# Attention layer: the root mean square of later queries and keys by a product with ones

## The chip, the cores and the metric

The kernel runs on one core of one Trainium2 chip. The metric is the device time of one execution in microseconds (us). The core has five engines that each work through a fixed list of instructions in order: TensorE (PE, matrix products; PEld is its weight load), VectorE (DVE), ScalarE (ACT), GpSimd (POOL), and SyncE (SP), which issues the loads and stores. They wait for each other by semaphores.

## What is computed

Two layers with d = 1024 over 512 latent tokens and 256 context tokens (T = 768). Layer 0 mixes tokens by grouped-query attention with 16 query heads and 4 key heads of 64 elements, layer 1 by a bidirectional state space scan; each is followed by a gated FFN. The change is in layer 0's attention:

```python
def rms_norm(x, g):
    y = x * lax.rsqrt(jnp.mean(x * x, axis=-1, keepdims=True) + EPS)     # EPS = 1e-6
    return y * g

q_l, k_l, v_l = jnp.split(h_lat @ w_qkv, [Q_DIM, Q_DIM + KV_DIM], axis=-1)
q_l = rms_norm(q_l.reshape(bsz, seq, N_HEADS, HEAD_DIM), q_norm)         # HEAD_DIM = 64
k_l = rms_norm(k_l.reshape(bsz, seq, N_KV_HEADS, HEAD_DIM), k_norm)
q_l, k_l = apply_rope(q_l, cos, sin), apply_rope(k_l, cos, sin)
...
s = einsum(q, k) * HEAD_DIM ** -0.5        # latent queries: all keys; context queries: context keys
o = softmax(s) @ v
```

So each query and key vector of 64 elements is scaled by the inverse root of its mean square, and its latent part is rotated by cos and sin. The result must be accurate to float32.

## The kernel before

Activations lie transposed: features on the 128 partitions, tokens along the free axis. A tile of queries holds two heads (64 partitions each) by 768 tokens, a tile of keys two key heads. Products that need float32 accuracy are done with a high and a low part (hi is a rounded copy made on ScalarE, lo the rest from VectorE or GpSimd: `split`, L85 and L87) and three products.

A *unit* is one such tile of queries or keys on its way from the projection to the scores. There are ten: keys 0 and 1, queries 0 to 7. Queries 0 to 3 and both keys come from projections in an earlier stage (tiles `raw`), queries 4 to 7 are projected in the unit itself (`queries`, tiles `qs`). The elementwise engine of a unit is given by `eng`: VectorE for keys 0 and queries 0, GpSimd for the other eight. The function `normed` does a unit's norm and rotation:

- ScalarE squares the tile (`qsq`, L523) and multiplies it by the gain (L524); four loads on SP's queue make a copy with rows exchanged in blocks of 32 (`qsw`, L527); `eng` does the rotation in three 512-wide steps (L528 to L530).
- `rstd_rows` (L226) then has PE multiply each 128 tokens of the squares with two indicator columns (`ssq`, six products, tokens on the partitions), VectorE and ScalarE form the inverse root on 128 x 12 elements (L239 to L244, one step of Newton behind Ln and Exp), VectorE spreads it over 128 x 768 (`rbq`, L247), PE transposes that in six pieces (`rsTq`, L253, four and two), and VectorE multiplies the tile with them (L534, 512 and 256).
- Queries end with hi (`qh`, ScalarE, L85) and lo (`ql`, VectorE, L87), keys with hi and lo copies for both halves of the partitions (L545 to L548).

The heads run as eight *pairs* (`Pair`), some 30 us each, from about 118 to 384 us. A pair has seven steps t: PE scores (`ps_s`, L668 with the correction `diag`, L670), ScalarE's exponential (`pr`, L671), VectorE's sum of exponentials (`acc`, `accc`), PE's products with the values one step later (`ps_o`, L632), at the end the sums with a tile of ones (`ps_sum`, `ps_oc`, L638), their inverse and the output (L641 to L645). In its steps the next pair's maxima are prepared too (`ps_m`, L596, reduced on VectorE, L598), and at its end these become the next pair's `diag` (`mz` L614, L619); so `qh` of pair p + 1 is needed in the first step of pair p's maxima run, which is the step t = 0 of pair p.

`ps_s` and `ps_m` share two PSUM buffers of two banks each; all other products (`Bk`) rotate through single banks.

Between the steps `Fill.run` (L182) pulls work from a list of generators, in the order queries 1, 2, 3, one ada, keys 1, query 4, and so on (`"123a4k5a6a7aaa"`, where `a` is a piece of the modulation, `ps_ada` and `ps_adt`). A generator yields an estimate of PE time, or `BREAK`, which costs 1 and rests it for three steps. `fill.require(qgen[p + 1])` at a pair's start runs what is left of the next queries. The program order that comes out is then placed on each engine by a scheduler, which keeps each engine's list in the order in which it expects the instructions to be ready.

The weights that are split during the heads (`wst`, `wh`, `wl`, and `wada` for the modulation) share one set of ten buffers of 128 x 1024 (`t4`), so a load on SP can wait for the reader of an older one.

Of the kernel before, what the change touches and what calls it, by code (L numbers as in the profile page):

```python
# [7 lines left out]
P = 128  # L8
F32 = mybir.dt.float32
F32R = mybir.dt.float32r  # L10
AF = mybir.ActivationFunctionType
ALU = mybir.AluOpType
# [5 lines left out]
L = 512  # L18
C = 256
T = L + C  # L20
HD = 64
# [4 lines left out]
EPS = 1e-6  # L26
# [41 lines left out]
def t3(g, name, dt=F32, n=T):  # L68
    return g.t3p.tile([P, n], dt, tag="t3", bufs=g.n3, name=name)
# [6 lines left out]
def _r(ap):  # L76

    return ap.bitcast(F32)


def split(g, src, hi, lo, lo_engine="dve", pin=False):

    nc = g.nc
    keep = g.tc.keep_in_program_order if pin else lambda i: i
    keep(nc.scalar.copy(hi, src))  # L85
    eng = nc.vector if lo_engine == "dve" else nc.gpsimd
    keep(eng.tensor_tensor(lo, src, _r(hi), ALU.subtract))  # L87
# [85 lines left out]
BREAK = object()  # L173
# [53 lines left out]
def rstd_rows(g, sq, n, cols, width, name, bank):  # L227

    nc = g.nc
    c = cols.shape[-1]
    nt = n // P
    ps = bank(f"ss{name}")
    for t in range(nt):
        nc.tensor.matmul(ps[:, t * c : (t + 1) * c], sq[:, t * P : (t + 1) * P], cols, start=True, stop=True)
    small = lambda nm: g.p.tile([P, nt * c], F32, tag="rst", bufs=8, name=nm)
    a, y, u = small("rsa"), small("rsy"), small("rsu")
    nc.vector.tensor_scalar(a, ps[:, : nt * c], 1.0 / width, EPS, ALU.mult, ALU.add)  # L239

    for f in ((lambda: nc.scalar.activation(y, a, AF.Ln)), (lambda: nc.scalar.activation(y, y, AF.Exp, scale=-0.5))):
        follow(g, f()) if g.tables else f()
    nc.vector.tensor_tensor(u, y, a, ALU.mult)
    nc.vector.scalar_tensor_tensor(u, y, -0.5, u, ALU.mult, ALU.mult)  # L244
    rb = t3(g, f"rb{name}", n=n)
    wide = lambda v: v.unsqueeze(2).broadcast_to([P, nt * c, P // c])
    nc.vector.scalar_tensor_tensor(rb.rearrange("p (a b) -> p a b", b=P // c), wide(u), 1.5, wide(y), ALU.add, ALU.mult)  # L247
    yield BREAK
    out = []
    for t0 in range(0, nt, 4):  # L250
        pt = bank(f"rsT{name}")
        for t in range(t0, min(nt, t0 + 4)):
            nc.tensor.transpose(pt[:, (t - t0) * P : (t - t0 + 1) * P], rb[:, t * P : (t + 1) * P], g.ident)  # L253
        yield (pt, t0 * P, min(n, (t0 + 4) * P))
# [124 lines left out]
def attention(g, fill, X, late):  # L379


    nc, I = g.nc, g.I
    S64 = slice(0, 64), slice(64, 128)
    Bk, Sb = (lambda name: Bank(g, name)), (lambda name: S(g, name))
# [48 lines left out]
    for m in range(KT):  # L433
        sq = t2("sql") if m else acc
# [7 lines left out]
    e = g.p.tile([P, 2 * KT], F32, name="silu")  # L442
# [20 lines left out]
    for m in range(KT):  # L463
# [5 lines left out]
        if m in (1, 2):  # L469
            for a in range(4 * m - 4, 4 * m):  # L470
                sq = t2("sqc")[:, :C] if a else sqc
# [35 lines left out]
    def values():  # L507
        for t in range(T // P):
# [7 lines left out]
                yield 0.32  # L516
            nc.scalar.copy(vt[t], ps[:, :256])


    def normed(qs, gain, eng):  # L520

        sq = t3(g, "qsq")
        nc.scalar.activation(sq, qs, AF.Square)  # L523
        nc.scalar.activation(qs, qs, AF.Identity, scale=gain)  # L524
        sw = t2("qsw")
        for b in range(4):
            nc.sync.dma_start(sw[32 * (b ^ 1) : 32 * (b ^ 1) + 32], qs[32 * b : 32 * b + 32, :L])  # L527
        eng.tensor_tensor(qs[:, :L], qs[:, :L], g.cos, ALU.mult)  # L528
        eng.tensor_tensor(sw, sw, g.sin, ALU.mult)
        eng.tensor_tensor(qs[:, :L], qs[:, :L], sw, ALU.add)  # L530
        for r in rstd_rows(g, sq, T, g.blk, HD, "q", Bk):
            if r is not BREAK:
                pt, c0, c1 = r
                nc.vector.tensor_tensor(qs[:, c0:c1], qs[:, c0:c1], pt[:, : c1 - c0], ALU.mult)  # L534
            yield BREAK
# [16 lines left out]
    qprep = {}  # L552

    def queries(p, qs, eng):
        if qs is None:
            w = load_w(g, I["wq"][p - 4], lo_engine="pool")
            yield BREAK
            qs = t3(g, "qs")
            for h, c0, n in ((hc, L, C), (hl, 0, L)):
                ps = Bk("ps_q")  # L560
                for k in range(KT):
                    ks = slice(k * P, (k + 1) * P)
                    mm3(g, (w[0][:, ks], w[1][:, ks]), [(ps[:, :n], h[k])], k == 0, k == KT - 1)
                    yield 3 * n / 2400
                nc.scalar.copy(qs[:, c0 : c0 + n], ps[:, :n])
            yield BREAK
        yield from normed(qs, g.qn8, eng)
        qprep[p] = t3(g, "qh", F32R), t3(g, "ql", F32R)
        split(g, qs, *qprep[p])
        yield 0  # L570

    onesr = g.const.tile([P, P], F32R, name="onesr")
# [6 lines left out]
    class Pair:  # L579
# [43 lines left out]
        def steps(self):  # L623

            (qh, ql), (kh, kl) = qprep[self.p], k2[self.kv]
            po = acc = None
            o = g.t3p.tile([P, T], F32, tag="o", bufs=2, name=f"o{self.p}")

            def values(po, pr, t, off, n, first, last):
                v = vt[t][:, self.kv * HD : (self.kv + 1) * HD]  # L630
                for e in range(2):
                    nc.tensor.matmul(po[S64[e], :n], v, pr[:, 512 * e + off : 512 * e + off + n], start=first, stop=last)  # L632

            def final(po, ps, acc, out):

                n = out.shape[-1]
                for e in range(2):
                    nc.tensor.matmul(ps[S64[e], :n], g.ones[:, :HD], acc[:, n * e : n * e + n], start=True, stop=True)  # L638
                y, u = t2("y")[:, :n], t2("u")[:, :n]

                nc.scalar.activation(y, ps, AF.Ln)  # L641
                nc.scalar.activation(y, y, AF.Exp, scale=-1.0)
                nc.vector.tensor_tensor(out, po, y, ALU.mult)
                nc.vector.scalar_tensor_tensor(u, ps, -1.0, y, ALU.mult, ALU.mult)
                nc.vector.scalar_tensor_tensor(out, u, 2.0, out, ALU.add, ALU.mult)  # L645

            def later_lat(po, pr, t, acc):
                values(po, pr, t, 0, L, t == 0, t == 5)
                if t == 5:
                    final(po, Bk("ps_sum"), acc, o[:, :L])  # L650

            def later_ctx(pr, acc):
                pc = Bk("ps_oc")
                for t in range(2):
                    values(pc, pr, 4 + t, C * t, C, t == 0, t == 1)
                final(pc[:, :C], pc[:, C:], acc, o[:, L:])
                if self.p < 6:
                    nc.sync.dma_start(odram[self.p], o)

            prev = None  # L660
            for t in range(7):
                ps, pr = Sb("ps_s"), g.t3p.tile([P, 1024], F32, tag="pr", bufs=3, name="pr")
                for q0, n, k0, off in (((0, L, t * P, 0),) if t < 6 else ((L, C, L, 0), (L, C, L + P, C))):
                    q, k = slice(q0, q0 + n), slice(k0, k0 + P)
                    outs = [ps[:, 512 * e + off : 512 * e + off + n] for e in range(2)]
                    for i, (a, b) in enumerate(((kh, qh), (kl, qh), (kh, ql))):
                        for e in range(2):
                            nc.tensor.matmul(outs[e], a[S64[e], k], b[S64[e], q], start=i == 0, stop=False)  # L668
                    for e in range(2):
                        nc.tensor.matmul(outs[e], onesr[S64[e]], self.diag[S64[e], q], start=False, stop=True)  # L670
                nc.scalar.activation(pr, ps, AF.Exp)  # L671
                if t == 0:
                    po = Bk("ps_o")
                elif t == 1:
                    acc = g.t3p.tile([P, 1024], F32, tag="acc", bufs=1, name="acc")
                    nc.vector.tensor_tensor(acc, prev, pr, ALU.add)
                elif t < 6:
                    nc.vector.tensor_tensor(acc, acc, pr, ALU.add)
                else:
                    acc = t2("accc")  # L680
                    halves = pr.rearrange("p (e k q) -> p e k q", e=2, k=2)
                    nc.vector.tensor_tensor(acc.rearrange("p (e q) -> p e q", e=2), halves[:, :, 0], halves[:, :, 1], ALU.add)
                prev = pr
                yield (lambda t=t, pr=pr, po=po, acc=acc: later_lat(po, pr, t, acc)) if t < 6 else (
                    lambda pr=pr, acc=acc: later_ctx(pr, acc))
            g.o.append(o)

    early = []
    for n, j in enumerate((0, 1, 2, 4, 5, 3)):
        ps = Bk("ps_c")  # L690
# [750 lines left out]
```

## Time and profile before

| | |
|---|---|
| Time, median of 3 runs | 1910.94 us (1908.98 to 1913.17) |
| Time of the profiled execution | 1905.24 us |
| Its span | 1903.5 us |
| TensorE busy | 1866.1 us (98%), 10796 products |
| VectorE busy | 1308.4 us (69%) |
| ScalarE busy | 822.8 us (43%) |
| GpSimd busy | 313.7 us (16%) |
| First scores of pairs 0 and 1 | 117.83 and 147.44 us |

Times in the profile are from one execution, in us unless ns is given, and L12 is line 12 of the kernel. A row of the groups reads: line, engine, operation, output and inputs, shapes, count, then busy time, mean ns of one, and the idle time of the engine before them with what ended it. A piece of the chain of waits reads: start, duration, engine, tile, line, count. In a row of waits stand the waiting engine and line, what it waited for, and total, times and longest.

### The profile page before, as it was taken

The numbers are of one execution on the slowest core, as the hardware profiler recorded it, in microseconds if no ns is written. First come the engines' busy times: TensorE is split into PE (matmuls) and PEld (weight loads), VectorE is DVE, ScalarE is ACT, GpSimd is POOL, SyncE is SP. The second block draws the span as 40 slices with busy tenths as digits, with TensorE's granted clock in tenths as the row PEclk, the third lists the DMA queues.
The fourth block names the chain that finished last, engine by engine and source line by source line (L and its number), as shares of the span: only waits on it lengthen the run. The fifth ranks groups of instructions, "written<-read, shape, count | busy, mean of one in ns | idle before, by whom it ended". The sixth has DMA issues, their size and how long they took to land.

```text
span 1903.5 us, 27436 instructions
## 1 busy us (share of the span) xinstructions
PE 1866.1 (98%) x10796; PEld 1540.9 (81%) x10796; DVE 1308.4 (69%) x1943; ACT 822.8 (43%) x1426; POOL 313.7 (16%) x274
## 2 busy tenths in 40 slices
PE   8999999999999999999989999999999999999999
PEld 6876555688888888888888888888888878888887
DVE  5578779678777777444487877777788466565555
ACT  3635344254122222222266677776666352323331
POOL 2241110030000000000040334444334210000000
PEclk8999999999999999999999999999999999999999
DMA  9221332115433554222223334434453223323232
GB/s 339 78 90 45 114 126 83 34 50 174 154 116 117 190 187 142 67 67 67 67 78 115 116 97 122 123 111 133 122 149 106 89 78 92 98 88 111 89 100 89
DMA packets 73425, 210.02 MB, mean 110 GB/s; under 512 B 8912, under 2 KB 14416, under 8 KB 73168
## 3 DMA queue, kind: packets, MB, share of 16 engines
q1 hardware_dynamic: 73296, 208.26, 34.6%
q8 instruction: 85, 1.39, 0.3%
q14 instruction: 44, 0.36, 0.1%
HBM read 198.79 MB, written 6.82 MB: 108 GB/s over the span
## 4 chain that ended last, share of the span: by engine, by line
PE 80%; DVE 10%; issue 3%; ACT 2%; POOL 1%; DMA 0%; DVEq 0%; POOLq 0%; ACTq 0%
PE ps_up L105 10%; PE ps_up L108 10%; PE ps_up L106 10%; PE ps_d L105 6%; PE ps_d L106 6%; PE ps_d L108 6%; PE ps_in L106 4%; PE ps_in L108 4%; PE ps_in L105 4%; PE ps_o L632 2%; PE ps_s L668 2%; PE ps_st L1028 2%; DVE ht L281 1%; PE ps_wo L108 1%; PE ps_wo L105 1%
## 5 line engine op out<-in xcount | busy, mean ns | idle before, releaser
L87 DVE TENSOR_TENSOR wl<-wst,wh 128x1024 fp32r<-128x1024 f32 x205 | 255.1, 1244 | 248.4 <-PE ps_up L106 137.3
L85 ACT CAST wh<-wst 128x1024 fp32r<-128x1024 f32 x211 | 221.3, 1049 | 429.2 <-DMA wst<-in_wup 346.3
L106 PE MATMUL ps_up<-hlf,wh 128*128 128x512 f32 x1008 | 357.0, 354 | 0.0
L105 PE MATMUL ps_up<-hhf,wh 128*128 128x512 f32 x1008 | 356.9, 354 | 0.0
L108 PE MATMUL ps_up<-hhf,wl 128*128 128x512 f32 x1008 | 356.8, 354 | 0.0
L105 PEld LDWEIGHTS ps_up<-hhf,wh 128*128 128x128 f32 x1008 | 190.6, 189 | 26.4
L108 PEld LDWEIGHTS ps_up<-hhf,wl 128*128 128x128 f32 x1008 | 190.5, 189 | 26.5
L106 PEld LDWEIGHTS ps_up<-hlf,wh 128*128 128x128 f32 x1008 | 190.6, 189 | 26.3
L105 PE MATMUL ps_in<-hhs,wh 128*128 128x512 f32 (+1 forms) x560 | 204.4, 365 | 0.0
L106 PE MATMUL ps_in<-hls,wh 128*128 128x512 f32 (+1 forms) x560 | 199.4, 356 | 0.0
L108 PE MATMUL ps_in<-hhs,wl 128*128 128x512 f32 (+1 forms) x560 | 198.7, 355 | 0.0
L105 PE MATMUL ps_d<-hdh,wh 128*128 128x512 f32 (+1 forms) x568 | 193.4, 342 | 1.4 <-DVE X L779 1.2
L108 PE MATMUL ps_d<-hdh,wl 128*128 128x512 f32 (+1 forms) x568 | 193.4, 341 | 0.0
L106 PE MATMUL ps_d<-hdl,wh 128*128 128x512 f32 (+1 forms) x568 | 192.8, 340 | 0.3 <-DVE hdl L87 0.3
L779 DVE SCALAR_TENSOR_TENSOR X<-ps_d,mod,X 128x512 f32<-128x512 f32 (+1 forms) x224 | 124.6, 583 | 36.7 <-PE ps_d L108 36.4
L106 PEld LDWEIGHTS ps_d<-hdl,wh 128*128 128x128 f32 x568 | 106.7, 188 | 14.8 <-DVE hdl L87 0.7
L105 PEld LDWEIGHTS ps_d<-hdh,wh 128*128 128x128 f32 x568 | 106.3, 188 | 14.8 <-DVE X L779 1.4
L105 PEld LDWEIGHTS ps_in<-hhs,wh 128*128 128x128 f32 x560 | 105.9, 189 | 15.2 <-issue 1.2
L108 PEld LDWEIGHTS ps_in<-hhs,wl 128*128 128x128 f32 x560 | 105.8, 189 | 14.7
L108 PEld LDWEIGHTS ps_d<-hdh,wl 128*128 128x128 f32 x568 | 106.7, 188 | 13.1
L106 PEld LDWEIGHTS ps_in<-hls,wh 128*128 128x128 f32 x560 | 106.0, 189 | 13.2
L671 ACT ACTIVATE pr<-ps_s 128x1024 f32<-128x1024 f32 x56 | 57.2, 1021 | 100.6 <-PE ps_s L670 99.6
(340 smaller groups left out, 3531.9 us busy)
## 6 DMA issues: line engine op xcount, KB each, us to landing
wst<-in_wup SPq DMA_DIRECT2D x88, 512.0 KB, 3.6
wada<-in_adaT SPq DMA_DIRECT2D x56, 512.0 KB, 3.7
wst<-in_win SPq DMA_DIRECT2D x48, 512.0 KB, 3.7
wst<-in_wdown SPq DMA_DIRECT2D x44, 512.0 KB, 3.7
E<-ad SPq DMA_DIRECT2D x64, 256.0 KB, 6.9
wada<-in_adaB SPq DMA_DIRECT2D x24, 512.0 KB, 4.7
ec<-ead SPq DMA_DIRECT2D x64, 128.0 KB, 5.4
wst<-in_wout SPq DMA_DIRECT2D x16, 512.0 KB, 3.6
```

The lines of the kernel that those rows point to most:

```text
L85: keep(nc.scalar.copy(hi, src))
L87: keep(eng.tensor_tensor(lo, src, _r(hi), ALU.subtract))
L105: mm(out, wh, ah, start=first, stop=False)
L106: mm(out, wh, al, start=False, stop=False)
L108: mm(out, wl, ah, start=False, stop=last)
L281: nc.vector.scalar_tensor_tensor(t[:, c0:c1], ap, g.moda[layer][ca][:, m, v : v + 1], rs[:, c0:c1], ALU.mult, ALU.mult)
L632: nc.tensor.matmul(po[S64[e], :n], v, pr[:, 512 * e + off : 512 * e + off + n], start=first, stop=last)
L668: nc.tensor.matmul(outs[e], a[S64[e], k], b[S64[e], q], start=i == 0, stop=False)
L671: nc.scalar.activation(pr, ps, AF.Exp)
L779: nc.vector.scalar_tensor_tensor(ap, o[:, c0:c1], gate[:, m, v : v + 1], ap, ALU.mult, ALU.add)
L1028: nc.tensor.matmul(ps[:, d * 256 : (d + 1) * 256], Bt[:, t * P : (t + 1) * P], xw[d][t], start=t == ts[0], stop=t == ts[-1])
```

## The change

For the eight units on GpSimd, `normed` leaves `rstd_rows` out. After the rotation it rests (`BREAK`). Then follow two `BREAK`s. The order of ScalarE's steps does not depend on GpSimd's.

Two orders are added by hand with `behind`: the products with the ones come behind the newest product with the values on PE at that point of the program (`scores["pe"]`), and the copy to `qh` behind the newest exponential on ScalarE (`scores["act"]`). Both set the order on one engine and add no wait.

```diff
--- before.py
+++ after.py
@@ -516,6 +516,17 @@
                 yield 0.32
             nc.scalar.copy(vt[t], ps[:, :256])
 
+    eps = g.const.tile([P, 1], F32, name="eps")
+    nc.gpsimd.memset(eps, EPS)
+    scores = {}
+
+    def behind(bi, engine):
+
+        if engine in scores:
+            g.tc.add_manual_dep(bi.ins, scores[engine].ins.name, mybir.DependencyInfo(
+                mybir.DependencyClass.NoSync, mybir.DependencyReason.DATA), reason="heads first")
+        return bi
+
 
     def normed(qs, gain, eng):
 
@@ -528,6 +539,27 @@
         eng.tensor_tensor(qs[:, :L], qs[:, :L], g.cos, ALU.mult)
         eng.tensor_tensor(sw, sw, g.sin, ALU.mult)
         eng.tensor_tensor(qs[:, :L], qs[:, :L], sw, ALU.add)
+        if eng is nc.gpsimd:
+
+
+            yield BREAK
+            a, y = t3(g, "qa"), t3(g, "qy")
+            for c in (slice(0, L), slice(L, T)):
+                ps = Bk("ssq")[:, : c.stop - c.start]
+                for h in S64:
+                    behind(nc.tensor.matmul(ps[h], g.ones[h, :HD], sq[h, c], start=True, stop=True), "pe")
+                nc.scalar.activation(a[:, c], ps, AF.Identity, scale=1.0 / HD, bias=eps)
+            u = sq
+            nc.scalar.activation(y, a, AF.Ln)
+            nc.scalar.activation(y, y, AF.Exp, scale=-0.5)
+            nc.scalar.activation(u, y, AF.Square)
+            eng.tensor_tensor(u, u, a, ALU.mult)
+            eng.tensor_scalar(u, u, -0.5, 1.5, ALU.mult, ALU.add)
+            eng.tensor_tensor(qs, qs, y, ALU.mult)
+            eng.tensor_tensor(qs, qs, u, ALU.mult)
+            yield BREAK
+            yield BREAK
+            return
         for r in rstd_rows(g, sq, T, g.blk, HD, "q", Bk):
             if r is not BREAK:
                 pt, c0, c1 = r
@@ -565,8 +597,9 @@
                 nc.scalar.copy(qs[:, c0 : c0 + n], ps[:, :n])
             yield BREAK
         yield from normed(qs, g.qn8, eng)
-        qprep[p] = t3(g, "qh", F32R), t3(g, "ql", F32R)
-        split(g, qs, *qprep[p])
+        qprep[p] = h, l = t3(g, "qh", F32R), t3(g, "ql", F32R)
+        behind(nc.scalar.copy(h, qs), "act")
+        nc.vector.tensor_tensor(l, qs, _r(h), ALU.subtract)
         yield 0
 
     onesr = g.const.tile([P, P], F32R, name="onesr")
@@ -629,7 +662,8 @@
             def values(po, pr, t, off, n, first, last):
                 v = vt[t][:, self.kv * HD : (self.kv + 1) * HD]
                 for e in range(2):
-                    nc.tensor.matmul(po[S64[e], :n], v, pr[:, 512 * e + off : 512 * e + off + n], start=first, stop=last)
+                    scores["pe"] = nc.tensor.matmul(po[S64[e], :n], v, pr[:, 512 * e + off : 512 * e + off + n],
+                                                    start=first, stop=last)
 
             def final(po, ps, acc, out):
 
@@ -668,7 +702,7 @@
                             nc.tensor.matmul(outs[e], a[S64[e], k], b[S64[e], q], start=i == 0, stop=False)
                     for e in range(2):
                         nc.tensor.matmul(outs[e], onesr[S64[e]], self.diag[S64[e], q], start=False, stop=True)
-                nc.scalar.activation(pr, ps, AF.Exp)
+                scores["act"] = nc.scalar.activation(pr, ps, AF.Exp)
                 if t == 0:
                     po = Bk("ps_o")
                 elif t == 1:
```

On the engines, in instructions with the control ones, PE has 8854 where it had 8864, VectorE 1678 for 1726, ScalarE 1107 for 1082, GpSimd 230 for 197, SP 244 for 245. In the new order of the heads: one of GpSimd's `wl` in pair 0 stands behind the rotation of queries 3; the `ssq` products of queries 6 stand behind the sums of pair 4; those of queries 7 behind the value products of pair 5's fifth step.

## The prediction

> **What bounds the kernel now.** I read the page first, then the waits of PE where the change works, then the chain of waits piece by piece around each norm.
>
> ```profile
> PE 1866.1 (98%) x10796; PEld 1540.9 (81%) x10796; DVE 1308.4 (69%) x1943; ACT 822.8 (43%) x1426; POOL 313.7 (16%) x274
> ```
>
> TensorE (PE) is busy 98% of 1903.5 us. A change elsewhere pays only where PE waits, or where PE itself gets less to do. The change touches eight norms of layer 0: the second keys (k1) and the queries of pairs 1 to 7 (q1 to q7), all between 80 and 310 us. PE's waits there, by line and releaser (us in total, times, longest):
>
> ```profile
> PE ps_m L596 <- DVE ma L598: 2.5, 4, 0.8
> PE rsTq L253 <- DVE rbq L247: 2.0, 1, 2.0
> PE ps_m L596 <- ACT qh L85: 1.0, 1, 1.0
> PE ps_s L670 <- DVE diag L619: 0.5, 2, 0.2
> PE ssq L236 <- ACT qsq L523: 0.3, 1, 0.3
> ```
>
> Together 6.3 us: all that a better order of waits could bring. Anything beyond must be PE work removed, and PE runs nearly without a gap otherwise, so any new lateness is paid in full. One 20 us window (width, then busy time of PE, PEld, DVE, ACT, POOL) shows where three norms are prepared in one head pair: VectorE (DVE) and GpSimd (POOL) are the full ones.
>
> ```profile
> 120.00:140.00 20.00, 18.80 (x133) 11.10 (x134) 18.46 (x24) 11.27 (x18) 13.22 (x8) 1.00 0.48 154
> ```
>
> **Part 1: PE work.** Before, a unit has six fp32 products of width 2 (12 records of ssq) and six transposes of rbq, in groups of 4 and 2. After, it has four fp32 products with the ones, two 64 x 512 and two 64 x 256, on diagonal quarters of the array. The nearest to these are the heads' sums, which use the same ones: a pair of 64 x 512 is four records, a pair of 64 x 256 too. Pieces of the chain (start, us), and two rows of the timeline for the group of 2:
>
> ```profile
> 145.21 0.86 PE ps_sum L638 x4
> ...
> 149.88 0.43 PE ps_oc L638 x4
> ...
> 175.39 1.43 PE ssq L236 x12
> ...
> 189.46 0.59 PE rsTq L253 x4
> ```
>
> ```profile
> 146.00 0.44 PE L253 MATMUL rsTq<-cst,rbq 128*128 128x128 f32 x2
> 146.19 0.36 PE L105 MATMUL ps_q<-hha,wh 128*128 128x256 f32 x1
> ```
>
> Removed: 1.43 + 0.59 + (146.19 - 146.00 = 0.19) = 2.21 us a unit. Added: 0.86 + 0.43 = 1.29, if the quarters overlap as the sums' two column halves do. Saving 0.92 x 8 = 7.4 us. Bounds: quarters one after the other, 2.58, a loss of 0.37 x 8 = 3.0; a 64-row product at half the sums' 128-row one, 0.65, a gain of 1.56 x 8 = 12.5. I take 7.4, because the sums have the same width, type and moving columns.
>
> What no row settles: ps_s has its two row halves in different PSUM banks, and ps_sum has its two column halves in one bank with all rows; the new quarters differ in rows and share a bank. The Trainium skill, "TensorEngine Tiling (Array Packing)", Gotcha 1: PSUM Pressure, says that different row tiles cannot access the same bank at once. By that the block takes 2.58 instead of 1.29 us, and the term is +3.0 instead of -7.4 (rival d).
>
> **Part 2: waits that go.** No product on PE needs the norm's scale any more, so the 2.0 us wait for rbq, in the values stage before pair 0, goes. VectorE loses, a unit, one each of L239, L243, L244, L247 and the two L534 products. The forms that carry it (count, total, mean ns):
>
> ```profile
> L243 DVE TENSOR_TENSOR rsu<-rsy,rsa 128x12 f32<-128x12 f32 x10 | 6.1, 612 | 3.3 <-ACT rsy L241 3.3
> L247 DVE SCALAR_TENSOR_TENSOR rbq<-rsu,rsy 128x768 f32<-128x768 f32 x10 | 11.7, 1166 | 0.4
> L534 DVE TENSOR_TENSOR raw<-raw,rsTq 128x512 f32<-128x512 f32 x6 | 4.1, 677 | 0.0
> ```
>
> That is 2.5 us a unit, so maxima come sooner. I give it 1.0 of the 2.8 us that PE waits for maxima and qsq, since the rest comes from the exclusion below, which grows. Waits won: 3.0 us.
>
> **Part 3: the new chain of a unit.** ScalarE (ACT) gets qa (512 + 256), Ln, Exp and Square (768); GpSimd gets three 768-wide products and one 768-wide operation with constants. Nearest rows:
>
> ```profile
> L523 ACT ACTIVATE qsq<-raw 128x768 f32<-128x768 f32 x6 | 5.0, 838 | 0.1
> L641 ACT ACTIVATE y<-ps_sum 128x512 f32<-128x512 f32 x6 | 3.6, 598 | 7.0 <-PE ps_sum L638 7.0
> ```
>
> ```profile
> L1061 POOL TENSOR_SCALAR_AFFINE_SELECT E<-E 128x512 f32<-128x512 f32 x64 | 65.9, 1052 | 71.5 <-DMA E<-ad 71.5
> L87 POOL TENSOR_TENSOR wsl<-wst,wsh 128x768 fp32r<-128x768 f32 x7 | 13.0, 1855 | 22.3 <-ACT wsh L85 22.1 <-POOL id L576 0.2
> ```
>
> ScalarE: 0.60 for 512, 0.84 for 768, so 0.24 for each 256 more and 0.36 for 256 alone: 0.60 + 0.36 + 2 x 0.84 = 2.64 us to y, Square 0.84 beside it. GpSimd: 3 x 1.86 + 1.05 x 768/512 = 1.5 (bounds: 1.05 and 1.86) = 7.1 us. The copy qh then costs 0.84 as before. So from the first 512 columns of ssq to qh: 2.64 + 7.1 + 0.84 = 10.6 us, and then maxima, mz and diag on VectorE. Before, the scale went over tiny 128 x 12 rows and VectorE. GpSimd works 8 x 7.1 = 57 us more, ScalarE 8 x 3.1 = 25 us; both are hidden by PE's work where the unit is early, and cost where it isn't. The four loads of qsw that a unit issues stay as they were.
>
> **Part 4: GpSimd and VectorE exclude each other.** A product of 128 x 12 with two inputs in SBUF took 2.08 us and ended with GpSimd's wl (121.30 + 2.37 = 123.67):
>
> ```profile
> 121.61 2.08 DVE L243 TENSOR_TENSOR rsu<-rsy,rsa 128x12 f32<-128x12 f32 x1 [0.64 <-ACT rsy L241]
> ```
>
> ```profile
> 121.30 2.37 POOL L87 TENSOR_TENSOR wl<-wst,wh 128x1024 fp32r<-128x1024 f32 x1 [0.67 <-ACT wh L85]
> 130.85 2.26 POOL L529 TENSOR_TENSOR qsw<-qsw,cs 128x512 f32<-128x512 f32 x1
> 133.18 1.30 POOL L530 TENSOR_TENSOR raw<-raw,qsw 128x512 f32<-128x512 f32 x1
> ```
>
> A 512-wide product on GpSimd takes 1.30 alone, 2.26 when VectorE's acc holds it up. acc, accc, mz, diag and ql have two such inputs; maxima, which read PSUM, do not wait. The Trainium skill, "SBUF — State Buffer", Who interferes with whom, says that the loser fully blocks, against any GpSimd instruction that reads SBUF; the row agrees for two-input ones, and no row shows the one-input kind. By it the 8 x 1.5 us of that kind exclude VectorE too; without it the late terms below shrink by 1.5 us at most each.
>
> **Where lateness reaches PE.** Pair 0's first scores (timeline), then pair 1's and the pieces of the chain that the terms below use:
>
> ```profile
> 117.83 0.50 PE L668 MATMUL ps_s<-qh,kh 64*128 64x512 f32 x2
> ```
>
> ```profile
> 147.51 0.89 PE ps_s L668 x5
> ...
> 254.84 1.43 PE ssq L236 x12
> ...
> 271.26 1.08 PE ps_oc L632 x8
> 272.35 0.43 PE ps_oc L638 x4
> ...
> 274.61 0.43 PE ps_m L596 x4
> ...
> 280.11 1.85 PE ps_ada L128 x16
> ...
> 301.62 1.03 DVE diag L619 x2
> ```
>
> Pair 0 to pair 1: 29.7 us (117.83 to 147.51). In it GpSimd now has two wl of 2.4, three sets of rotary products of 3 x 1.3 (two queries and k1), and 7.1 for q1's norm: 23.6 us, plus 5 to 8 us in which acc and the like shut it out (four to six of 1.2 to 1.3), so 28.6 to 31.6, and qh behind it at 29.5 to 32.5, then ql, and diag. PE, three blocks of 0.92 shorter and with the wait of 0.8 for a maximum partly gone, would be there at 26.5 to 28, and the first exponential, no longer covered by an ssq block, costs it 0.9. One of the wl now stands behind a rotary set on GpSimd, and an ada load on SP's queue waits for it, with the next wq load behind: a wh cast on ScalarE, which is ahead of qa and an exponential, can be late by up to 2.5 us. Stall 2 to 8 us; I take 4.5, and 0.9.
>
> q2 to q5 and k1 stand 10 to 20 us ahead of their use, more than the chain of 10.6: nothing but 0.6 us for collisions.
>
> q6: its ssq stood at 254.84, far ahead of ps_m at 274.61. Held behind the heads' products, it is issued after pair 4's last sum. Cover on PE behind it: the second ssq 0.43, scores 0.89 (as at 147.51) and some 0.2 for diag, the context's values and sums 1.0 + 0.43, two ps_ada of 1.85, half a ps_o 0.5 = 7.2 us against 10.6, with ps_m standing in PE's order behind. Stall 3.4, with the exponential between Exp and Square 0.5 more, and ql (0.95), now ahead of the maxima on VectorE, 0.95: 4.9 (bounds 3 and 6).
>
> q7: its ssq falls into pair 5's fifth step with less PE work behind it. qh stands in ScalarE's order ahead of pair 6's first exponential; accc, mz, diag and wl alternate with GpSimd's steps, so that diag, before at 301.62, is late as well. Stall 5.3 to 7 less the 1.0 that stood there: 5 (bounds 3 and 6).
>
> Sum: -7.4 - 3.0 + 0.9 + 4.5 + 0.6 + 4.9 + 5.0 = +5.5 us. No weight load is nearer behind the heads, so it is carried to the end. The profiled execution has 1905.24 us around its span of 1903.5, so 1910.7; the median of the runs shown, 1910.94, is 5.7 above it. Forecast 1910.94 + 5.5 = 1916.
>
> **The rivals.** (a) Faster: a stall is partly paid back. While PE waits, VectorE and ScalarE catch up, so the wait for maxima (2.5) goes wholly and the late terms count half: -7.4 - 2.0 - 2.8 + 0.9 + 7.2 = -4.1, 1907. For it: DVE is relieved by 8 x 2.5 us. Against: qh and diag are on one chain that nothing else shortens. (b) No change: GpSimd's list in pair 0 isn't shut out, so the 4.5 falls away: +1, 1912. For it: maxima aren't blocked. Against: 18.46 us of DVE in that window. (c) Slower, from one place: the wq load behind wl comes 2.5 us late and both diag and qh of pair 1 follow; 8 + 6 + 6 at the three places instead of 14.4, +11, 1922. It decides if GpSimd reaches that wl later than its wada buffer is free. (d) The quarters run one after the other because they share a bank: each of eight blocks takes 2.58, the PE term turns from -7.4 to +3.0, the total to +15.9, 1927. For it: no row has two row halves at work in one bank. Against: their output partitions differ, like those of the sums. (e) The hold does nothing because ssq stays as far ahead as before: q6 and q7 cost 1 instead of 9.9, -3.4, 1907.5. Against: the order of q6's products has them behind the sums.
>
> **How the numbers follow.** Forecast 0.43 (own range 1912 to 1921), (a) 0.14, (b) 0.15, (c) 0.13, (d) 0.09, (e) 0.06. About 0.2%, 3.8 us, is what a measurement can tell from no change. Of the forecast's 0.43, 0.12 lies within it; (a) and (e), at -4.1 and -3.4, lie on its edge and give 0.14 to faster and 0.06 to the same; a little of (b), 0.02, goes to slower. Faster 0.14; some 0.04 more for a block of ones as cheap as its lower bound (0.65), taken from the forecast: 0.18. Same 0.12 + 0.06 + 0.13 = 0.31, less 0.02 of these, 0.29. Slower 0.43 - 0.12 - 0.02 + 0.02 + 0.13 + 0.09 = 0.53. The range, 1905 to 1925, leaves out (d), the outer end of (c) and a part of (a).
>
> **What would show it.** Right: a PE wait for qh of 3 to 5 us near 270 and one near 300, and 2 to 8 near 147; ssq blocks of about 1.3 us; rsTq gone; acc and the like longer beside GpSimd's 768-wide steps. Wrong: ssq blocks of 2.6, no wait for qh, or a pair 1 that starts as early as its PE work allows.

## The result and the profile after

The changed kernel takes 1930.74 us (median of 6 runs, 1928.23 to 1933.41) against 1910.81 (6 runs, 1907.73 to 1914.82): ratio 1.0104, 95% interval 1.0092 to 1.0116. It is 19.9 us slower, where 5.5 were forecast.

The page's first part, and PE's waits between 80 and 330 us (total us, times, longest):

```profile
PE 1867.5 (97%) x10716; PEld 1534.0 (80%) x10716; DVE 1311.6 (68%) x1895; ACT 846.1 (44%) x1450; POOL 370.6 (19%) x307
```

```profile
PE ps_s L704 <- DVE diag L652: 20.3, 5, 7.1
PE ps_m L629 <- ACT qh L601: 4.0, 2, 3.0
PE ps_s L702 <- ACT pr L705: 3.4, 4, 1.5
PE ps_s L702 <- DVE ma L631: 0.9, 1, 0.9
```

Before, these waits came to 6.3 us; now to 28.6, and 20.3 of them are for `diag`, which VectorE forms at the end of each head pair from `mz`. The wait for rbq is gone. The groups of these two operations in the same stretch, before and then after (count, total, mean ns):

```profile
L619 DVE TENSOR_TENSOR diag<-id,mz 128x384 fp32r<-128x384 f32 x14 | 7.2, 554 | 0.2
L614 DVE TENSOR_TENSOR mz<-ma,mb 64x6 f32<-64x6 f32 x28 | 5.5, 196 | 0.4
```

```profile
L647 DVE TENSOR_TENSOR mz<-ma,mb 64x6 f32<-64x6 f32 x28 | 16.2, 580 | 0.4
L652 DVE TENSOR_TENSOR diag<-id,mz 128x384 fp32r<-128x384 f32 x14 | 11.2, 843 | 0.1
```

Operations on six columns have become three times as long. The end of pair 0 shows how; VectorE's timeline, then GpSimd's, then PE's:

```profile
142.53 1.97 DVE L716 TENSOR_TENSOR accc<-pr 128x512 f32<-128x512 f32 x1
144.42 4.45 DVE L647 TENSOR_TENSOR mz<-ma,mb 64x6 f32<-64x6 f32 x4
148.91 0.96 DVE L602 TENSOR_TENSOR ql<-raw,qh 128x768 fp32r<-128x768 f32 x1
149.78 2.63 DVE L652 TENSOR_TENSOR diag<-id,mz 128x384 fp32r<-128x384 f32 x2
```

```profile
136.65 1.83 POOL L558 TENSOR_TENSOR raw<-raw,qy 128x768 f32<-128x768 f32 x1
...
142.13 1.82 POOL L559 TENSOR_TENSOR raw<-raw,qsq 128x768 f32<-128x768 f32 x1
143.91 2.27 POOL L558 TENSOR_TENSOR raw<-raw,qy 128x768 f32<-128x768 f32 x1
146.15 1.79 POOL L556 TENSOR_TENSOR qsq<-qsq,qa 128x768 f32<-128x768 f32 x1
148.03 0.83 POOL L557 TENSOR_SCALAR qsq<-qsq 128x768 f32<-128x768 f32 x1
148.95 2.58 POOL L559 TENSOR_TENSOR raw<-raw,qsq 128x768 f32<-128x768 f32 x1
```

```profile
152.46 0.80 PE L704 MATMUL ps_s<-diag,onesr 64*128 64x512 f32 x2 [7.09 <-DVE diag L652]
153.05 0.63 PE L629 MATMUL ps_m<-kh,qh 64*128 64x256 f32 x4
153.61 1.97 PE L665 MATMUL ps_oc<-pr,v 128*64 128x256 f32 x8
```

accc can run only when the step of 142.13 has ended (143.95), the first mz when that of 143.91 has (146.18), the second when that of 146.15 has (147.94): the engines alternate, one operation each, however short. Taken one by one, the four mz last 1.78, 1.75, 0.16 and 0.70 us: the third slips in between two steps, the fourth ends with the one-input step (148.86). Together they take 4.45 us instead of some 0.7, and diag meets the last step. The first of the two norms (queries of pair 2, from 136.65) has ended before mz and holds up only accc; it is the second one (queries of pair 3, from 143.91), for which nobody is in a hurry, that runs beside mz and diag. PE stands for 7.09 us. The end of pair 1 shows the same (VectorE, GpSimd). There one mz waits for the second keys' last step, and two wait for the rotation of pair 4's queries, which the kernel before has too; there it held up one mz (1.22 us):

```profile
182.59 4.43 DVE L647 TENSOR_TENSOR mz<-ma,mb 64x6 f32<-64x6 f32 x4
187.05 1.98 DVE L652 TENSOR_TENSOR diag<-id,mz 128x384 fp32r<-128x384 f32 x2
```

```profile
182.22 2.15 POOL L559 TENSOR_TENSOR raw<-raw,qsq 128x768 f32<-128x768 f32 x1
184.33 1.25 POOL L539 TENSOR_TENSOR qs<-qs,cs 128x512 f32<-128x512 f32 x1
185.55 1.25 POOL L540 TENSOR_TENSOR qsw<-qsw,cs 128x512 f32<-128x512 f32 x1
186.88 1.27 POOL L541 TENSOR_TENSOR qs<-qs,qsw 128x512 f32<-128x512 f32 x1
```

A second cost follows each of the four waits of 3 us and more: behind it PE runs at half its clock. Windows of the changed kernel (width, then busy time of PE, PEld, DVE, ACT, POOL; the third number from the end is the granted clock):

```profile
145.00:149.00 4.00, 0.37 (x4) 0.00 (x0) 3.91 (x5) 1.21 (x3) 3.83 (x4) 1.00 0.00 0
149.00:152.00 3.00, 0.00 (x0) 0.00 (x0) 3.00 (x3) 0.00 (x0) 2.52 (x1) 0.52 0.01 3
152.00:156.00 4.00, 3.54 (x18) 2.08 (x18) 3.51 (x6) 1.02 (x1) 0.00 (x0) 0.50 0.00 0
156.00:160.00 4.00, 4.00 (x23) 2.04 (x20) 2.60 (x5) 1.82 (x3) 0.00 (x0) 1.00 0.19 75
```

The eight products of ps_oc at 153.61 take nearly twice the 1.08 of before (at 271.26, in the prediction's chain). Summed over windows of 2 us from 90 to 420 us, PE's busy time times (1 - granted clock) is 7.4 us after and 1.7 before.

Finally, one block of the products with the ones, in the chain of waits:

```profile
172.07 1.44 PE ssq L550 x8
```

So from the first product of the values to the last pair's context values, 294.2 us before and 314.2 after, the 20.1 us are made of: gaps of more than 0.1 us between PE's products 28.8 - 6.6 = +22.3; half clock 7.4 - 1.7 = +5.7; products -7.9 (not measured by itself: it is what is left, with all else that is in neither of the two). The span differs by 23.0; 1.7 of it lies ahead of the first product of the values, whose start varies from 89.8 to 93.6 us over the profiles of all kernels here, and 1.2 behind the heads.

### The profile page after: what moved, and what is told of

The parts are those of the page before. It is cut to its first block, busy times and chain, and to the rows that moved or that the text cites. A ratio compares the mean times of both kernels' runs of the same rounds, so it can differ in the third digit from the quotient of the medians.

```text
span 1926.5 us, 27324 instructions
## 1 busy us (share of the span) xinstructions
PE 1867.5 (97%) x10716; PEld 1534.0 (80%) x10716; DVE 1311.6 (68%) x1895; ACT 846.1 (44%) x1450; POOL 370.6 (19%) x307
## 4 chain that ended last, share of the span: by engine, by line
PE 78%; DVE 9%; issue 4%; ACT 3%; POOL 2%; DMA 1%; DVEq 0%; POOLq 0%; ACTq 0%
PE ps_up L106 10%; PE ps_up L105 10%; PE ps_up L108 10%; PE ps_d L105 6%; PE ps_d L106 6%; PE ps_d L108 6%; PE ps_in L108 4%; PE ps_in L106 4%; PE ps_in L105 4%; PE ps_s L702 2%; PE ps_o L665 2%; PE ps_st L1062 2%; DVE ht L281 1%; PE ps_wo L108 1%; PE ps_wo L105 1%
## 5 line engine op out<-in xcount | busy, mean ns | idle before, releaser
L108 PEld LDWEIGHTS ps_d<-hdh,wl 128*128 128x128 f32 x568 | 106.7, 188 | 13.1
L330 POOL TENSOR_TENSOR sqs<-sqs 128x256 f32<-128x256 f32 x15 | 11.2, 745 | 523.8 <-issue 516.4
```

The source lines that it names most:

```text
L108: mm(out, wl, ah, start=False, stop=last)
L330: (nc.vector if m == 7 else nc.gpsimd).tensor_tensor(acc, acc, sq, ALU.add)
```

## The experiments

Theory 1: GpSimd's 768-wide steps and VectorE's operations of two inputs in SBUF exclude each other, and it costs where the tiny mz and diag of a pair's end meet such steps. Theory 2: the new norm is held too long, so its chain is late. Ratios are to the kernel before, with 95% intervals.

| run | median, us | ratio (interval) |
|---|---|---|
| vec4 | 1922.8 | 1.0058 (1.0041 to 1.0075) |
| vec3 | 1915.6 | 1.0027 (1.0015 to 1.0038) |
| thirds | 1930.3 | 1.0099 (1.0077 to 1.0120) |
| no_hold | 1932.4 | 1.0110 (1.0089 to 1.0132) |
| extra_two_input | 1920.6 | 1.0050 (1.0031 to 1.0069) |
| extra_one_input | 1912.7 | 1.0001 (0.9986 to 1.0016) |
| extra_write_only | 1910.3 | 0.9989 (0.9977 to 1.0002) |
| one_step | 1913.5 | 1.0012 (0.9997 to 1.0026) |
| vec3_rot | 1912.5 | 1.0006 (0.9990 to 1.0022) |
| vec3_no_hold | 1917.1 | 1.0032 (1.0019 to 1.0045) |
| vec3_rot_early | 1915.2 | 1.0020 (1.0008 to 1.0032) |
| vec3_rot_early_no_hold | 1918.2 | 1.0040 (1.0025 to 1.0055) |
| after_diag | 1926.5 | 1.0078 (1.0054 to 1.0101) |
| after_diag_rest | 1923.3 | 1.0064 (1.0043 to 1.0085) |
| hybrid | 1916.3 | 1.0035 (1.0021 to 1.0049) |
| hybrid_rest | 1918.8 | 1.0042 (1.0028 to 1.0055) |
| hybrid_early | 1922.4 | 1.0059 (1.0037 to 1.0082) |

### The hold, and where the steps run

no_hold:

```diff
-        if engine in scores:
+        if False:
```

> The two hand-made orders (products with the ones behind the heads' products, qh's copy behind the exponential) are left out. Theory 1: GpSimd's steps meet the pairs' ends as before, PE's wait for diag stays at 12 to 22 us, time 1924 to 1934. Theory 2: the chain starts earlier and the time falls to 1911 to 1917.

1932.4 us, the same as with the hold within the intervals, and PE's waits for diag stay (total, times, longest), and so do those for qh:

```profile
PE ps_s L704 <- DVE diag L652: 17.5, 5, 5.4
...
PE ps_m L629 <- ACT qh L601: 4.0, 2, 3.0
```

The hold is not the cause; theory 2 in this form falls.

vec4 and vec3 move the four steps to VectorE, vec3 as three:

```diff
-            eng.tensor_tensor(u, u, a, ALU.mult)
-            eng.tensor_scalar(u, u, -0.5, 1.5, ALU.mult, ALU.add)
-            eng.tensor_tensor(qs, qs, y, ALU.mult)
-            eng.tensor_tensor(qs, qs, u, ALU.mult)
+            nc.vector.scalar_tensor_tensor(u, u, -0.5, a, ALU.mult, ALU.mult)
+            nc.vector.tensor_tensor(qs, qs, y, ALU.mult)
+            nc.vector.scalar_tensor_tensor(qs, u, 1.5, qs, ALU.add, ALU.mult)
```

> The four 768-wide steps of the later norms run on VectorE instead of GpSimd; the rest as in the changed kernel. Theory 1 (exclusion: at the pairs' ends the tiny mz and diag on VectorE each wait for a 768-wide GpSimd step): PE's wait for diag, 20.3 us before pair 6 in the changed kernel, falls under 5 us, and the time to 1908 to 1914 us, although VectorE does 3.9 us a unit more. Theory 2 (the norm's chain is simply issued too late because it is held): the chain gets shorter by 3 us only (4 x 1.0 instead of 7.1), three late places win 3 us each, 1920 to 1925.

> The norm's last steps are three fused ones on VectorE (2.9 us a unit) instead of four on GpSimd. Theory 1: PE's wait for diag under 4 us, time 1904 to 1911, as PE has 6 us less of products than before the change. Theory 2: 1918 to 1924.

vec3 wins back 15.1 of the 19.9 us, vec4 8.0. In vec4 the wait for diag is 6.1 us; both are slower than theory 1 had them, and vec4's time lies in theory 2's range. In vec3 PE still waits 7.3 us for diag, 3.6 of it at the end of pair 1, where the rotation of pair 4's queries, still on GpSimd, meets mz (VectorE, then GpSimd):

```profile
176.96 2.75 DVE L646 TENSOR_TENSOR mz<-ma,mb 64x6 f32<-64x6 f32 x4
179.73 2.09 DVE L651 TENSOR_TENSOR diag<-id,mz 128x384 fp32r<-128x384 f32 x2
```

```profile
177.18 1.28 POOL L539 TENSOR_TENSOR qs<-qs,cs 128x512 f32<-128x512 f32 x1 [10.61 <-ACT qs L596]
178.42 1.25 POOL L540 TENSOR_TENSOR qsw<-qsw,cs 128x512 f32<-128x512 f32 x1
179.75 1.66 POOL L541 TENSOR_TENSOR qs<-qs,qsw 128x512 f32<-128x512 f32 x1
```

vec3_rot moves the rotation to VectorE as well:

```diff
-        eng.tensor_tensor(qs[:, :L], qs[:, :L], g.cos, ALU.mult)
-        eng.tensor_tensor(sw, sw, g.sin, ALU.mult)
-        eng.tensor_tensor(qs[:, :L], qs[:, :L], sw, ALU.add)
+        nc.vector.tensor_tensor(qs[:, :L], qs[:, :L], g.cos, ALU.mult)
+        nc.vector.tensor_tensor(sw, sw, g.sin, ALU.mult)
+        nc.vector.tensor_tensor(qs[:, :L], qs[:, :L], sw, ALU.add)
```

> The norm's three fused steps and the rotation too on VectorE, so that in the heads only GpSimd's splits of weights are left. Theory 1 (the 7.3 us of waits for diag that stay with the norm on VectorE are from the rotation on GpSimd): waits for diag under 2.5 us; but VectorE does 2.0 us a unit more where it is nearly full, so maxima come later; time 1908 to 1917. Rival (VectorE's own load makes diag late): waits for diag 7 to 12 us, 1917 to 1923.

1912.5 us, no difference to the kernel before that can be told. The mean mz is now 159 ns, and diag is back at 554; but 4.2 us of wait for diag, more than theory 1 had, and 3.6 for qh stay. So the exclusion is not all; that the rest is VectorE's own load is argued, not shown.

### The size of a step, and how many

thirds:

```diff
-            eng.tensor_tensor(u, u, a, ALU.mult)
+            for c in thirds:
+                eng.tensor_tensor(u[:, c], u[:, c], a[:, c], ALU.mult)
...
```

> Each of the four GpSimd steps is cut into three of 256 columns. Theory 1: a tiny VectorE step that loses waits 0.6 to 0.9 us instead of 1.8, so PE's wait for diag falls from 20.3 to 8 to 13 us, time 1918 to 1925. Theory 2 (late chain): GpSimd's chain gets longer by the fixed cost of eight more instructions a unit, so no gain, 1930 to 1936.

The waits for diag fell by 7.4 us, as theory 1 said, but the chain got longer, and 3.2 came back as waits for qh. All waits of this stretch are 24.5 us where they were 28.6, and the half clock, summed as above, costs 11.9 where it cost 7.4. So the time did not move: theory 1's range is missed, and 1930.3 lies in theory 2's.

```profile
PE ps_s L709 <- DVE diag L657: 12.9, 5, 4.2
PE ps_m L634 <- ACT qh L606: 7.2, 3, 4.0
```

one_step leaves one of the four steps:

```diff
-            nc.scalar.activation(u, y, AF.Square)
-            eng.tensor_tensor(u, u, a, ALU.mult)
-            eng.tensor_scalar(u, u, -0.5, 1.5, ALU.mult, ALU.add)
             eng.tensor_tensor(qs, qs, y, ALU.mult)
-            eng.tensor_tensor(qs, qs, u, ALU.mult)
```

> The changed kernel with one of GpSimd's four steps (the tile times y) and without ScalarE's Square; Newton's correction is left out, so the norm is as exact as Ln and Exp are. Theory 1: GpSimd's added work falls from 7.1 to 1.9 us a unit, and PE's waits for diag from 20.3 to 3 to 9 us, time 1910 to 1917. Theory 2 (held too late): q6 and q7 get 5 us each from the shorter chain, waits for diag between the other pairs stay: 1920 or more.

1913.5 us and 6.8 us of wait for diag: inside theory 1's bounds, below theory 2's. One new wait, 4.5 us at 140 for an exponential, stands beside them.

### The exclusion by itself

Three kernels are the one before with four idle GpSimd operations behind each later unit's rotation: products of two inputs, an operation of one input, memsets.

```diff
+        if eng is nc.gpsimd:
+            extra = t3(g, "extra")
+            for _ in range(4):
+                eng.tensor_tensor(extra, sq, sq, ALU.mult)
```

> The kernel before, with four idle 768-wide GpSimd products of two inputs behind each later unit's rotation (nobody waits for their result). It has the old norm, with nothing held. Theory 1 (exclusion with VectorE's tiny steps): maxima, mz and diag come late, PE's waits for VectorE between 80 and 380 us rise by 6 to 18 us, time 1918 to 1930 us. Theory 2 (late chain of the new norm): 1910 to 1913.

> The same with four idle GpSimd operations of one input and two constants. Theory 1 with the rule that any GpSimd step that reads SBUF excludes: as with two inputs but for the shorter step (0.83 instead of 1.83 us), waits up by 3 to 9 us, 1914 to 1921. If only two-input steps exclude: 1910 to 1913.

> The same with four idle GpSimd memsets of 768 columns, which read nothing. Theory 1 with that rule: no new waits, 1910 to 1913. If GpSimd's being busy or its writes already hinder: as with one input, 1914 or more.

The extra operation, diag and mz in each (mean ns in the second place), first with two inputs, then with one, then with none:

```profile
L534 POOL TENSOR_TENSOR extra<-qsq 128x768 f32<-128x768 f32 x32 | 53.7, 1680 | 78.6 <-ACT qsq L523 76.8
```

```profile
L623 DVE TENSOR_TENSOR diag<-id,mz 128x384 fp32r<-128x384 f32 x14 | 10.4, 783 | 0.2
L618 DVE TENSOR_TENSOR mz<-ma,mb 64x6 f32<-64x6 f32 x28 | 9.5, 341 | 0.4
```

```profile
L534 POOL TENSOR_SCALAR extra<-qsq 128x768 f32<-128x768 f32 x32 | 34.2, 1070 | 76.9 <-ACT qsq L523 74.9
```

```profile
L618 DVE TENSOR_TENSOR mz<-ma,mb 64x6 f32<-64x6 f32 x28 | 6.4, 229 | 0.4
```

```profile
L534 POOL MEMSET extra<- 128x768 f32 x32 | 23.6, 739 | 3.4 <-PE ps_c L108 2.1
```

```profile
L618 DVE TENSOR_TENSOR mz<-ma,mb 64x6 f32<-64x6 f32 x28 | 5.5, 196 | 0.4
```

Idle work of two inputs, whose result nobody reads, costs 9.4 us, half of what the change costs; so the old norm, with nothing held, pays too. In its profile, of an execution 4.0 us over the median, PE's waits between 80 and 330 us add up to 12.1 against 6.3, none of them for a result of GpSimd, and the half clock costs 8.1 against 1.7: about half of what this execution lost is the clock behind these waits. Memsets leave mz at the 196 ns of before and cost nothing. That is how the Trainium skill, "SBUF — State Buffer", Who interferes with whom, has it: GpSimd instructions that read SBUF exclude VectorE's of two SBUF inputs, those that only write do not. One input takes 1.07 us here where it took 0.83 undisturbed (148.03 above), so it is kept out as well, and the fourth mz at 148.17 waited for such a step; but its cost was no more than the measurement can tell: the 1914 to 1921 expected for it were too high.

### The place

after_diag delays the second keys' and pair 3's steps by two rests and starts them when the diag of the pair then ending is done:

```diff
+            for _ in range(late):
+                yield BREAK
...
+            if late:
+                for s in steps[:2]:
+                    g.tc.add_manual_dep(s.ins, held["diag"].ins.name, mybir.DependencyInfo(
+                        mybir.DependencyClass.Sync, mybir.DependencyReason.DATA), reason="after diag")
```

> The changed kernel, with GpSimd's four steps for the queries of pair 3 and the second keys begun only when the diag of the pair then ending is done, so that they no longer run beside mz and diag; their work, and everything else, is the same. Theory 1 (the cost lies where these steps meet mz and diag): the waits for diag near 152 (7.1 us) and 189 (4.9 us) fall to 1 to 3 us each and the clock stays whole there, time 1917 to 1923 us. If the steps cost the same wherever they run (any exclusion, or GpSimd's load as such): 1928 to 1933 us.

At the end of pair 0 the same steps now start at 147.46, behind diag, and mz and diag are as short as alone (VectorE, GpSimd):

```profile
144.70 0.69 DVE L651 TENSOR_TENSOR mz<-ma,mb 64x6 f32<-64x6 f32 x4
145.42 0.96 DVE L606 TENSOR_TENSOR ql<-raw,qh 128x768 fp32r<-128x768 f32 x1
146.30 1.02 DVE L656 TENSOR_TENSOR diag<-id,mz 128x384 fp32r<-128x384 f32 x2
```

```profile
147.46 1.83 POOL L558 TENSOR_TENSOR raw<-raw,qy 128x768 f32<-128x768 f32 x1 [3.23 <-DVE diag L656]
149.26 1.84 POOL L558 TENSOR_TENSOR qsq<-qsq,qa 128x768 f32<-128x768 f32 x1
```

The waits there fell from 7.1 to 1.6 us and from 4.9 to under 0.7 (at the second place the rotation of pair 4's queries has moved away too, to 186.95), and the clock stays whole up to 280 us. The time, 1926.5, still misses theory 1's 1917 to 1923: the rests pushed projections into the last pairs, and PE waited 8.8 us for pair 7's qh. after_diag_rest takes the rests' cost out of the estimate that pulls in projections:

```diff
-                yield BREAK
+                yield REST
...
+                if r is REST:
+                    self.cool[g] = 3
```

> As after_diag, but the two rests that delay the units of the second keys and of pair 3 take nothing from the estimate with which the heads pull in projections, so that the other units' projections stay where they are in the changed kernel. Theory 1 (place): 1915 to 1922 us, with waits for diag near 152 and 189 under 3 us and those of pairs 4 to 6 as in the changed kernel. If the amount of GpSimd's work counts: 1926 to 1932 us.

1923.3 us, 7.5 less than the changed kernel, with the same GpSimd work, and 1.3 above theory 1's bounds. Its wait for diag up to 200 us is 4.1, where it was 13.6; the 5.4 at the last unit stays. So the place of two units' steps is worth 7.5 us with the amount unchanged. It does not show that the amount costs nothing in the 12.5 us that stay, which hold the untouched last two units.

### Looking for a version that gains

All of these keep the products with the ones. vec3_no_hold is vec3 with `if False`, vec3_rot_early is vec3_rot without the rest ahead of the products with the ones, the third is both:

> The three fused steps on VectorE, without the two hand-made orders. Theory 1: the hold is worth little either way, 1913 to 1918 (1915.6 with it). Theory 2, now for what is left with VectorE: waits for qh (2.4) and part of those for diag (7.3) go, 1908 to 1912.

> Three fused steps and the rotation on VectorE, and the rest before the products with the ones left out, so that a unit's chain starts about three steps of a pair earlier. If what is left of waits there (qh 3.6, diag 4.2, pr 2.9) is lateness of the chain: 1905 to 1909. If it is VectorE's load: 1911 to 1915 (1912.5 with the rest).

> As the one before, also without the two hand-made orders. Lateness: 1904 to 1908. VectorE's load: 1911 to 1915.

1917.1, 1915.2 and 1918.2 us; the second and third lie above both of their ranges. With the steps on VectorE the hold is no loss (1915.6 with it, 1917.1 without), and an earlier start gains nothing. But that does not clear lateness: in vec3_rot_early's profile the waits for diag and qh are 2.6 and 1.0 us, where vec3_rot had 4.2 and 3.6, and PE waits for the squares instead:

```profile
PE ssq L548 <- ACT qsq L534: 3.5, 2, 2.9
```

So the wait moved from one end of the chain to the other. hybrid, hybrid_rest and hybrid_early take vec3's steps for pairs 1, 2, 6 and 7 and after_diag's for the rest:

```diff
+            if vec:
+                nc.vector.scalar_tensor_tensor(u, u, -0.5, a, ALU.mult, ALU.mult)
...
+        yield from normed(qs, g.qn8, eng, 2 if p == 3 else 0, p in (1, 2, 6, 7))
```

> As the one before, and the queries of pairs 1, 2, 6 and 7, which are late or in the values stage, take the three fused steps on VectorE; GpSimd keeps the second keys and the queries of pairs 3, 4 and 5. Theory 1: most waits for diag and qh go (under 6 us together) and PE's 7 to 8 us less of products show: 1904 to 1911 us. If the rest is VectorE's load: 1912 to 1917 us.

> As hybrid, with the same rests without cost. Theory 1 (place, and lateness for the last two units): the loss of the last pairs in hybrid goes, 1904 to 1911 us. VectorE's load: 1912 to 1917 us.

> As hybrid_rest, and the queries of pairs 6 and 7 leave out the rest before their products with the ones, so that these start three steps earlier. If the last two units are late: 2 to 5 us faster than hybrid_rest. If not: the same within 2 us.

1916.3, 1918.8 and 1922.4 us. hybrid lies in the range given for VectorE's load, the other two above all that was expected; neighbours' intervals overlap, and the earlier start, for which 2 to 5 us of gain were expected, brought none. In hybrid_rest's profile 13.1 us of gaps and 4.7 of half clock are left, ten pieces over 0.7 us among them and none over 2.3 us, so no one wait could be named. No version beat the kernel before.

## Why the prediction was wrong

The direction was right and the exclusion was named, but the sum was +5.5 where 19.9 was measured, outside the range of 1905 to 1925.

- PE's products: -7.4 predicted. The block is 1.44 us instead of 1.29, so by the prediction's own rows (2.21 - 1.44) x 8 = 6.2 us are saved; the -7.9 above is a remainder and no check. The quarters do overlap although they share a bank (rival d falls), against the Trainium skill's rule in "TensorEngine Tiling (Array Packing)", Gotcha 1, which the prediction weighed: 1.44 and not 2.58.
- Waits that go: -3.0 predicted. The wait for rbq went (2.0), and that for maxima fell from 2.5 to 0.9. Right.
- New waits: +15.9 predicted. The waits left after what goes were to be 6.3 - 3.0 + 15.9 = 19.2; they are 28.6. **The step that failed:** "q2 to q5 and k1 stand 10 to 20 us ahead of their use, more than the chain of 10.6: nothing but 0.6 us for collisions." A unit that is early is safe as to its qh, but its GpSimd steps harm whichever pair's end they pass. That is 5.5 us at 152 (what after_diag takes off the 7.1) and 4.9 at 189. Another 3.0 stand in three pieces at 213 to 223; pair 4's steps run there until 213.89, but the last piece, 1.3 us, comes behind a wl of GpSimd beside accc and ql ahead of diag, so not all of it is theirs. For pair 0 the text counted one norm, called q1's, whose qh would be late. Two ran there (q2's and q3's; q1's had run in the values stage). q2's qh was ready at 144.83, before PE stopped at 145.37; diag was late, in the main behind the second, early norm. That the 7.1 lies within the 2 to 8 given for this place is luck. The start of pair 0 added 2.4 where 0.9 was taken (diag 1.5, pr 0.9).
- q6 was right in kind (qh late behind GpSimd) and smaller, 3.0 for 4.9, but the hold is not the reason: without it (no_hold) the products with the ones stand behind the same sums, and the wait is the same 3.0. q7 cost 5.4 + 1.5 where 5 was taken, in diag and not in qh.
- The work was sized right for GpSimd (370.6 us busy, 56.9 more, where 57 were taken). VectorE, from which 2.5 us a unit were taken off, got busier by 3.2 us, since an operation that GpSimd holds up counts as busy.
- Missing altogether: the half clock after the long waits, +5.7. The row was there: before, the clock is 0.50 behind the 2.0 us wait in the values stage.

```profile
104.00:107.00 3.00, 3.00 (x16) 3.00 (x15) 2.10 (x4) 0.83 (x1) 0.00 (x0) 0.50 0.00 0
```

With the two, 5.5 + (28.6 - 19.2) + 5.7 - 0.5 = 20.1, the lengthening of the heads; the -0.5 is the remainder's difference from -7.4, so the sum closes by construction.

- The rivals: (a) and (e), faster, (b) and (d) are excluded, though (e) had one half right: the hold does nothing, but the products with the ones stand late without it too. (c), the wq load late, happened but wasn't it: ScalarE's wh waited 1.44 us for that load, up to 136.06, and PE's gap behind it, at 139.91, is 0.23 us.

Shown by runs: GpSimd's steps that read two inputs cost time also when nobody waits for their result (extra_two_input); with the amount of work unchanged, moving two units' steps away from mz and diag wins 7.5 us (after_diag_rest); taking the steps off GpSimd wins 15.1 (vec3). Not settled: why the versions with the steps on VectorE still gain nothing from the fewer products, and lose up to 12 us (vec4, whose profile is of an execution 4.5 us over its median). Summed as above, vec3 has gaps of 15.6 and half clock of 5.7 us, vec3_rot 14.0 and 2.5, against 6.6 and 1.7 before: the saving goes into short waits and the clock behind them, and what causes each of these is open.

## What to carry to other kernels

Short operations that many wait for, such as a reduction's last combine, should not stand beside long elementwise steps of an engine with which theirs excludes: each tiny one can wait for a whole long one, and of four in a row three did. Work moved off a busy engine is not free because the other engine is idle; look for what the other's instructions will stand beside, also when the work itself is early. And a new wait on PE can cost more than its length: the clock stayed at half for 3.5 us behind the wait of 7.1, and in all the half clock added 5.7 us to 22.3 of gaps.

## What the runs showed of the hardware

The granted clock fell to 0.50 some 4 us into a wait of 7.1 us and stayed there for 6.8 us, to 156 us, 3.5 of them behind the wait; before, it fell behind a wait of only 2.0 us and stayed for 3.4. The Trainium skill, "TensorE: Matmul & The Clock Gate", Part 1, gives an idle window of some 3.4 us for it to fall; the slow stretches, once and twice that long, agree with it, but the 2.0 us wait is shorter than that window, so there the measurement decides. The length of a wait alone does not settle it either: at the start of pair 0 the clock stayed at 1.00 in after_diag (118 to 128 us), with waits of 1.7 and 0.9 us, and was 0.50 in after_diag_rest (120 to 126 us), with waits of 1.7 and 0.7 us.

Memsets of 768 columns beside VectorE's two-input operations left these at 196 and 554 ns, as in the kernel before, while steps that read two inputs raised them to 341 and 783 ns, in otherwise equal kernels.
